# Block products in the first feed-forward layer as well, modulation rows moved, border squares summed by products, two output tiles together in the recurrent output: a float32 decoder trunk on one core

## Chip, cores, metric

One core of one Trainium2 chip. The metric is the time of one launch on the device in microseconds; the median of several runs counts. All inputs lie in device memory, the output is written there.

## What is computed

Two layers over a sequence of 512 tokens, model width 1024. Layer 0 mixes by sparse attention, layer 1 by a gated recurrent unit; each is followed by a feed-forward block of 22 x 128 = 2816 hidden units. Everything is float32.

```python
def swiglu(h, w_in, w_out):
    g, u = jnp.split(h @ w_in, 2, axis=-1)
    return (jax.nn.silu(g) * u) @ w_out

def reference(x, c, ada_w, ada_b, ...):
    cond = jax.nn.silu(c)
    for layer in range(DEPTH):
        mod = (cond @ ada_w[layer] + ada_b[layer])[:, None, :]
        sh1, sc1, g1, sh2, sc2, g2 = jnp.split(mod, 6, axis=-1)
        hh = rms_norm(x, norm1_g[layer]) * (1.0 + sc1) + sh1
        ...
        x = x + g1 * mix        # mix: nsa_mixer in layer 0, rglru_mixer in layer 1
        hh = rms_norm(x, norm2_g[layer]) * (1.0 + sc2) + sh2
        x = x + g2 * swiglu(hh, ffn_w_in[layer], ffn_w_out[layer])
    return x
```

## The kernel before

Activations lie transposed: `x` is eight tiles of 128 features x 512 tokens. Every float32 factor is split into a high part and a low rest of a reduced type (`split`, L244), and a product is three matmuls, high x high, high x low, low x high (`mm3`, L256 to L261). A weight tile of 128 x 1024 is loaded raw into one of four buffers `wraw` (`raw`, L216), ScalarE makes the high halves (L248), DVE or POOL the low ones (L254), into six buffers each. `chunk` (L230) does both halves and then `behind` (L223), which issues up to `per_chunk` modulation rows of a list `todo`.

A **modulation row** (`ada`, L264) is one of 96 tiles of 512 KB of `ada_w`: its load goes through `raw`, DVE multiplies it by the broadcast condition and sums (L271), and adds a bias of 128 x 1 (L272).

The program in order: `setup` (condition, masks); `nsa`, which starts with the squares of `x`, the normalising scale (`norm_scale`, L298: sums of squares by small products L309, a power on POOL L278, a diagonal L318, its broadcast by PE L320) and a loop over the eight input tiles (L601) with 24 products of 512 columns for each; then the selection and compression branches and attention, with the last output projection in token halves (`w_out_last`, L1080) as the border to the next block; `ffn(0)`; `rg`; `ffn_blocks(1)`.

The plain `ffn` (L520) takes hidden tiles in pairs (gate and value), 24 products of 512 columns each, Silu at L540. `ffn_blocks` (L377) computes a pair by a two-by-two block scheme with seven products in place of eight: 7 x 4 x 3 = 84 matmuls of 256 columns. `load(j)` (L398) brings the pair's two raw tiles `v` and `g` and makes sums and differences on DVE (L404 to L407); `run(i, j)` (L418) does one of the seven products, with its weight split just before, and the outputs are put together on DVE (L430, L444 to L450). Silu of the first half stands at L431. The right operands are made once per layer by `right_operands` (L354, differences L360). Two pairs at the head are done whole, since the blocks need all of the operands.

`project_out` (L547) multiplies the hidden tiles by the output weights; with `ahead` = 2 the first two output tiles are done together, hidden tile by hidden tile. `sq_add` (L281) squares a finished tile on ScalarE and adds it to the running sum on POOL, except those in `apart`, which stay for a product of their own.

A scheduler sets the order on each engine from the order of the program and the numbers in `PRIORITY` (L122); an engine works its list in order, and loads are issued by SP in the order of its own list.

Of the kernel before, what the change touches and what calls it, by code (L numbers as in the profile page):

```python
# [105 lines left out]
class Build:  # L106
    def __init__(self, ctx, tc, ins, out):
# [15 lines left out]
        "ada1": -140, "ada2": -20, "ck": -60, "cmp": -60, "comb": 90, "exp": -170, "fill": -6, "first2": -40,  # L123
        "first4": -20, "gates": -60, "gproj": -25, "krms": -20, "kt": 60, "late": 30, "lo": -300, "max": 20,
        "mod1": -100, "mod2": 40, "mod3": -66, "nsc1": -41, "nsc2": -40, "pres3": -20, "psplit": 10, "pv": 15,
# [36 lines left out]
    def setup(self):  # L162
        nc, c = self.nc, self.const
        row = self.raw(self.ins["c"], D)[:1]
        self.load_x()
        self.vec = c.tile([128, NVEC], F32, name="vec")
        nc.sync.dma_start(self.vec, self.ins["vec"])
        self.ones = c.tile([128, 128], F32, name="ones")
        nc.vector.memset(self.ones, 1.0)
        nc.scalar.activation(row, row, AF.Silu)  # L170
        self.cond = c.tile([128, D], F32, name="cond")
        for h in range(2):
            b = self.bank()
            nc.tensor.matmul(b, self.ones[:1], row[:, 512 * h:512 * h + 512], start=True, stop=True)
            nc.scalar.activation(self.cond[:, 512 * h:512 * h + 512], b, AF.Copy)
        self.mhalf = c.tile([128, 16], F32, name="mhalf")
# [26 lines left out]

    def load_x(self, behind=None):
        self.x = []
        for n in range(KT):
            self.x.append(self.slot("A", name="x"))
            d = self.nc.sync.dma_start(self.x[n], self.ins["x"][:, n])
            if behind is not None:
                self.after(d.ins, behind.ins.name)  # L210

# [51 lines left out]

    def ada(self, l, m, n, engine):  # L264
# [5 lines left out]
        w = self.raw(self.ins["ada_w"][l, KT * m + n], D)  # L270
# [26 lines left out]
    @step("nsc")  # L297
    def norm_scale(self, cs=ALL, behind=None):  # L298

# [18 lines left out]
        nc.vector.tensor_tensor(dg, self.ident[:, None, :].to_broadcast([128, nt, 128]),  # L318
                                r[:, :, None].to_broadcast([128, nt, 128]), op=OP.mult)
        nc.tensor.matmul(R[:, :w], self.ones, dg.rearrange("p a b -> p (a b)"), start=True, stop=True)  # L320
        return R[:, :w]

    def hh_tile(self, n, R, A, B, cs=ALL, to=None, t=None):
        nc = self.nc
        if t is None:
            t = self.slot("T")[:, cs]
        nc.vector.tensor_tensor(t, self.x[n][:, cs], R, op=OP.mult)
# [21 lines left out]

    BLOCKWISE = ((1, 2),)  # L350
    kept = {}
# [25 lines left out]
    def ffn_blocks(self, l, last):  # L377
# [20 lines left out]
        def load(j):  # L398
# [4 lines left out]
            with self.pri("wsum"):  # L403
# [48 lines left out]


        plain = dict(zip((0, HT, 1), self.first(src, (0, HT, 1))))
        if l == 0:
            self.rg_prepare()
        w = self.chunk(src[HT + 1], 1024)
        self.right_operands()
        plain[HT + 1] = self.bank()
        for k in range(KT):  # L460
            self.mm3(plain[HT + 1], w[128 * k:128 * k + 128], self.hh[k], k == 0, k == KT - 1)
        for j in (0, 1):
# [12 lines left out]
        run(4, HT - 1)  # L475
        self.flush((l, 5))
        for j in range(HT):
# [69 lines left out]
    def project_out(self, src, h, gate, then, ahead=1):  # L547
# [34 lines left out]
    def nsa(self):  # L582
        nc, tc = self.nc, self.tc
        for n in range(KT):
            self.sq_add(n, nc.vector, apart=(6,))
        for m in (0, 1):
            last = self.ada(0, m, 0, nc.vector)
        R = self.norm_scale(behind=last)
        with tc.tile_pool(name="nsa", bufs=1) as np_:
            self.np_ = np_  # L590

            self.K = {g: [self.slot("K", F32R, f"K{g}", self.KW) for _ in range(2)] for g in range(GROUPS)}
            self.V, self.qs, self.oT, self.cells, self.ends = {}, {}, {}, [], []
# [7 lines left out]
            for k in range(KT):  # L601
                for m in (0, 1) if k else ():
                    self.ada(0, m, k, nc.vector)
                A = self.make_A(0, 1, slice(k, k + 1))
                hh.append(self.hh_tile(k, R, A, self.mod[0, 0]))
                w = self.chunk(self.ins["nsa_w1"][k], 1024, "ag")
                for t in range(4):
                    s = slice(128 * t, 128 * t + 128)
                    self.mm3(cb[t], w[s], hh[k], k == 0, k == KT - 1)
                for i in range(NT):  # L610
                    s = slice(128 * i, 128 * i + 128)
                    self.mm3(wb[i], (hh[k][0][:, s], hh[k][1][:, s]),
                             w[512:1024], k == 0, k == KT - 1)
            self.todo += [(0, m, n) for m in (2, 4, 3) for n in range(KT)]
            self.behind_on = nc.vector
# [464 lines left out]
    def w_out_last(self, cs):  # L1080
# [3 lines left out]
        for n in range(KT):  # L1084
# [37 lines left out]
    def rg(self):  # L1122
        nc, tc = self.nc, self.tc
        src = self.ins["rg_in"]
        early = dict(zip((RT, RT + 1, RT + 2), self.first(src, (RT, RT + 1, RT + 2))))

# [204 lines left out]
```

## Time and profile before

| | |
|---|---|
| median of 3 runs | 1368.15 us (1366.61 to 1369.36) |
| profiled execution | 1366.38 us, its span 1364.5 us |
| PE busy | 1306.9 us, 96%, 7423 instructions |
| PE weight loads | 1113.4 us, 82% |
| DVE busy | 931.2 us, 68% |
| ScalarE busy | 702.6 us, 51% |
| POOL busy | 239.8 us, 18% |
| mean granted TensorE clock | 0.991 |

The span runs from the first to the last instruction of the profiled execution; 1.9 us of its time lie around it. By the trace the loop over the input tiles of attention runs from 23 to 72 us, the border from 384 to 411, `ffn(0)` from 407 to 766, the recurrent block to 1011 and `ffn_blocks(1)` to the end. A matmul's printed time overlaps the next one's, so the distance of starts is what a stream of them costs. A clock of 1.00 stands for 2.4 GHz, 0.5 for 1.2 GHz.

### The profile page before, as it was taken

How to read it: one execution, taken by the hardware profiler on the slowest of the kernel's cores; microseconds unless marked ns; L12 is line 12 of the kernel's file. 1: busy time of each engine (PE TensorE's matmuls, PEld its weight loads, DVE VectorE, ACT ScalarE, POOL GpSimd, SP SyncE). 2: the span in 40 equal slices, each digit the busy share in tenths (PEclk: the TensorE clock that was granted, in tenths of full speed). 3: DMA queues.
4: the chain of work that ended last, by engine and by line, in shares of the span. 5: the costliest groups of instructions: out<-in, count | busy, mean ns of one | idle time of the engine just before them, and what ended most of it. 6: DMA issues, size and time to landing. Idle time of an engine off the chain costs nothing.

```text
span 1364.5 us, 20521 instructions
## 1 busy us (share of the span) xinstructions
PE 1306.9 (96%) x7423; PEld 1113.4 (82%) x7423; DVE 931.2 (68%) x1883; ACT 702.6 (51%) x1605; POOL 239.8 (18%) x334
## 2 busy tenths in 40 slices
PE   5989988899989999999999999999999999999998
PEld 4789866667769888888888987787898999998887
DVE  7885987888877566566533577478369888887331
ACT  4473588888665333333222555595366555556221
POOL 3540334586341000000000013300110000000000
PEclk9999999999999999999999999999999999999999
DMA  7667600210214666666643123222322333334430
GB/s 261 227 189 241 218 21 1 92 64 17 84 56 140 215 201 203 194 191 191 196 131 101 63 85 93 93 93 85 101 78 89 98 97 118 96 96 126 123 112 24
DMA packets 50071, 167.20 MB, mean 123 GB/s; under 512 B 5553, under 2 KB 6833, under 8 KB 49970
## 3 DMA queue, kind: packets, MB, share of 16 engines
q1 hardware_dynamic: 49970, 165.90, 39.3%
q8 instruction: 58, 0.95, 0.3%
q14 instruction: 43, 0.35, 0.1%
HBM read 163.78 MB, written 2.10 MB: 122 GB/s over the span
## 4 chain that ended last, share of the span: by engine, by line
PE 77%; DVE 11%; issue 4%; ACT 4%; DMA 2%; POOL 2%; POOLq 0%; SPq 0%; ACTq 0%; DVEq 0%
PE bank_tr L259 9%; PE bank_tr L260 9%; PE bank_tr L261 9%; PE bank_sc L259 7%; PE bank_sc L260 7%; PE bank_sc L261 7%; PE bank_mm L259 4%; PE bank_mm L260 4%; PE bank_mm L261 4%; PE bank_pv L261 3%; PE bank_pv L259 2%; PE bank_pv L260 2%; PE bank_tr L1046 2%; PE bank_pv L1059 2%; DVE wraw L271 2%
## 5 line engine op out<-in xcount | busy, mean ns | idle before, releaser
L248 ACT ACTIVATE whi<-wraw 128x512 fp32r<-128x512 f32 (+4 forms) x422 | 245.4, 594 | 424.0 <-PE bank_tr L260 152.4
L254 DVE TENSOR_TENSOR wlo<-wraw,whi 128x512 fp32r<-128x512 f32 (+3 forms) x390 | 254.3, 658 | 183.4 <-ACT whi L248 174.2
L271 DVE SCALAR_TENSOR_TENSOR wraw<-wraw,cond 128x1024 f32<-128x1024 f32 x96 | 119.1, 1241 | 73.9 <-DMA wraw<-in_ada_w 73.5
L259 PE MATMUL bank_tr<-hh,whi 128*128 128x512 f32 (+1 forms) x400 | 137.3, 344 | 5.3 <-ACT hh L248 3.0
L261 PE MATMUL bank_tr<-hh,wlo 128*128 128x512 f32 (+1 forms) x400 | 135.5, 339 | 1.8 <-DVE wlo L254 1.8
L260 PE MATMUL bank_tr<-hh,whi 128*128 128x512 f32 (+1 forms) x400 | 136.3, 341 | 0.1
L295 POOL TENSOR_TENSOR sq<-sq 128x256 f32<-128x256 f32 (+1 forms) x25 | 25.9, 1034 | 432.2 <-ACT sq L286 431.8
L261 PE MATMUL bank_sc<-hh,wlo 128*128 128x512 f32 (+1 forms) x284 | 101.1, 356 | 0.0
L259 PE MATMUL bank_sc<-hh,whi 128*128 128x512 f32 (+1 forms) x284 | 101.1, 356 | 0.0
L260 PE MATMUL bank_sc<-hh,whi 128*128 128x512 f32 (+1 forms) x284 | 101.1, 356 | 0.0
L259 PEld LDWEIGHTS bank_tr<-hh,whi 128*128 128x128 f32 x400 | 76.5, 191 | 17.8 <-ACT hh L248 4.7
L261 PEld LDWEIGHTS bank_tr<-hh,wlo 128*128 128x128 f32 x400 | 76.6, 192 | 10.0 <-DVE wlo L254 2.0
L260 PEld LDWEIGHTS bank_tr<-hh,whi 128*128 128x128 f32 x400 | 76.7, 192 | 8.8 <-DVE hh L254 0.6
L1011 DVE TENSOR_REDUCE nm<-bank_sc 128x1 f32<-128x32 f32 (+4 forms) x192 | 69.5, 383 | 14.1 <-PE bank_sc L970 8.3
L995 POOL TENSOR_SCALAR p<-p,rr 128x128 f32<-128x128 f32 (+3 forms) x128 | 66.4, 539 | 45.5 <-DVE rr L986 36.6
L1014 ACT ACTIVATE p<-bank_sc,nm 128x384 f32<-128x384 f32 (+3 forms) x128 | 67.2, 531 | 11.6 <-DVE nm L1011 10.9
L248 ACT ACTIVATE ph<-bank_tr 128x512 fp32r<-128x512 f32 (+1 forms) x96 | 56.0, 595 | 14.6 <-PE bank_tr L1046 13.4
L1046 PE MATMUL bank_tr<-ident,p 128*128 128x128 f32 x320 | 55.1, 276 | 5.9 <-DVE ph L254 4.9
L261 PEld LDWEIGHTS bank_sc<-hh,wlo 128*128 128x128 f32 x284 | 53.9, 190 | 8.0 <-DVE wlo L254 0.4
L259 PEld LDWEIGHTS bank_sc<-hh,whi 128*128 128x128 f32 x284 | 53.9, 190 | 7.6 <-ACT whi L248 0.2
L260 PEld LDWEIGHTS bank_sc<-hh,whi 128*128 128x128 f32 x284 | 53.8, 189 | 7.5
L254 POOL TENSOR_TENSOR wlo<-wraw,whi 128x512 fp32r<-128x512 f32 (+1 forms) x44 | 53.4, 1227 | 32.9 <-ACT whi L248 32.5
(429 smaller groups left out, 3712.2 us busy)
## 6 DMA issues: line engine op xcount, KB each, us to landing
wraw<-in_ada_w SPq DMA_DIRECT2D x96, 512.0 KB, 4.2
wraw<-in_ffn_in SPq DMA_DIRECT2D x88, 512.0 KB, 3.7
wraw<-in_ffn_out SPq DMA_DIRECT2D x32, 512.0 KB, 3.6
wraw<-in_rg_in SPq DMA_DIRECT2D x22, 512.0 KB, 3.3
wraw<-in_ffn_out SPq DMA_DIRECT2D x16, 384.0 KB, 3.1
x<-in_x SPq DMA_DIRECT2D x16, 256.0 KB, 3.9
wraw<-in_nsa_w SPq DMA_DIRECT2D x8, 512.0 KB, 4.5
wraw<-in_cmp_w SPq DMA_DIRECT2D x8, 512.0 KB, 5.1
```

The costliest lines, as they stand in the source:

```text
L248: nc.scalar.activation(hi, full, AF.Copy)
L254: e.tensor_tensor(lo, full, hi.bitcast(F32), op=OP.subtract)
L259: a = mm(out, w[0], x[0], start=first, stop=False)
L260: mm(out, w[0], x[1], start=False, stop=False)
L261: return a, mm(out, w[1], x[0], start=False, stop=last)
L271: done = engine.scalar_tensor_tensor(w, w, 1.0, self.cond, op0=OP.mult, op1=OP.mult, accum_out=mod)
L295: engine.tensor_tensor(s, s, t, op=OP.add)
L995: nc.gpsimd.tensor_scalar(P[br, h], P[br, h], r[:, h, x:x + 1], 1.0, op0=OP.mult, op1=OP.mult)
L1011: nc.vector.tensor_reduce(nm[:, h, x:x + 1], b[:, cols[br]] if len(brs) > 1 else b, axis=AX, op=OP.max, negate=True)
L1014: nc.scalar.activation(dst, b[:, cols[br]] if len(brs) > 1 else b, AF.Exp, bias=nm[:, h, x:x + 1], accum_out=sm[:, h, x:x + 1])
L1046: nc.tensor.transpose(t[:n, 128 * h:128 * h + 128], srcs[h], self.ident)
L1059: mm(o, V[:, g], ph, start=first and u == 0, stop=False)
```

## The change

- `ffn_blocks(0)` takes the place of `ffn(0)`. Both layers now do three pairs whole (`PLAIN`), and the first two block pairs are interleaved. Layer 0 issues a modulation row with every odd pair; in layer 1 none are left.
- The start: two modulation rows load among the tiles of `x`, into the eight `K` buffers; the squares are summed by PE alone; products of no use (`warm`) run on PE ahead of the first ones needed; the low halves of the loop over input tiles move from POOL to DVE.
- The border: `w_out_last` keeps squares 2 to 7 apart, so PE sums them by products.
- `per_chunk` is 0 in most of `rg`, and 1 in the gate projection and from the third output tile on; the recurrent output is called with `ahead` = 2.

```diff
 def setup(self):
-        self.load_x()
+        self.x, self.early = [], []
+        for n in range(KT):
+            self.x.append(self.slot("A", name="x"))
+            nc.sync.dma_start(self.x[n], self.ins["x"][:, n])
+            if n >= KT - 2:
+                self.early.append(self.raw(self.ins["ada_w"][0, KT * (n - KT + 2)], D, True))
...
+        nc.scalar.activation(self.cond[:, 0:1], self.ones[:, 0:1], AF.Silu)
+        self.warm(8, self.ones)
...
+    def warm(self, n, src):
+        for _ in range(n):
+            self.nc.tensor.matmul(self.idle_bank[:, :128], self.ones, src[:, :128], start=True, stop=True)
...
-    def raw(self, src, w):
-        t = self.wp.tile([128, 1024], F32, name="wraw", bufs=4)
+    def raw(self, src, w, wide=False):
+        t = self.slot("K", name="adaw", w=1024) if wide else self.wp.tile([128, 1024], F32, name="wraw", bufs=4)
...
 def norm_scale(self, cs=ALL, behind=None, warm=None):
...
+        if warm:
+            self.after(d.ins, warm[0].ins.name)
+            self.warm(warm[1], parts[-1])
+        m = nc.tensor.matmul(R[:, :w], self.ones, dg.rearrange("p a b -> p (a b)"), start=True, stop=True)
...
-    BLOCKWISE = ((1, 2),)
+    BLOCKWISE = ((0, 2), (1, 2))
+    PLAIN = (3, 3)
...
-            if j % 2:
+            if j % 2 and l == 0:
                 self.behind()
...
+        n = self.PLAIN[l]
...
-        for j in range(2, HT):
+        load(n)
+        run(1, n)
+        run(2, n)
+        load(n + 1)
+        for i, j in ((1, n + 1), (2, n + 1), (5, n), (6, n), (3, n), (7, n), (5, n + 1), (4, n), (6, n + 1), (3, n + 1),
+                     (7, n + 1)):
+            run(i, j)
+        for j in range(n + 2, HT):
             load(j)
             for i in (1, 2, 5):
                 run(i, j)
-            if j > 2:
-                run(4, j - 1)
+            run(4, j - 1)
             for i in (6, 3, 7):
                 run(i, j)
         run(4, HT - 1)
-        self.flush((l, 5))
...
 def project_out(...):
+            self.per_chunk = 1 if n0 > 1 or K > 16 else 0
...
 def nsa(self):
-            self.sq_add(n, nc.vector, apart=(6,))
-        for m in (0, 1):
-            last = self.ada(0, m, 0, nc.vector)
-        R = self.norm_scale(behind=last)
+            self.sq_add(n, nc.vector, apart=range(1, KT))
+        first, last = [self.ada(0, m, 0, nc.vector, self.early[m]) for m in (0, 1)]
+        R = self.norm_scale(behind=first, warm=(last, 6, 0))
...
-                    self.ada(0, m, k, nc.vector)
+                    d = self.ada(0, m, k, nc.vector, self.raw(self.ins["ada_w"][0, KT * m + k], D, True))
...
-                w = self.chunk(self.ins["nsa_w1"][k], 1024, "ag")
+                w = self.chunk(self.ins["nsa_w1"][k], 1024)
...
 def w_out_last(self, cs):
-            self.sq_add(n, self.nc.gpsimd, cs)
+            self.sq_add(n, self.nc.gpsimd, cs, range(2, KT))
...
 def rg(self):
+        self.per_chunk = 0
...
+        self.per_chunk = 1
         with self.pri("gproj"):
             gb = [project(j) for j in range(8)]
+        self.per_chunk = 0
...
-        self.project_out(self.ins["rg_out"][0], y, self.mod[1, 2], (1, 2))
+        self.project_out(self.ins["rg_out"][0], y, self.mod[1, 2], (1, 2), 2)
...
-        self.ffn(0, False)
+        self.ffn_blocks(0, False)
```

How it moves instructions, at three places. First DVE at the start, from the last sum of squares to the first scaled tile; L271, L287 multiply a modulation row, `nv` is the mean square, L318, L334 the diagonal. Before:

```order
L295 TENSOR_TENSOR sq<-sq 128x512 [waits DVE_49,Activation_49] x4
L295 TENSOR_TENSOR sq<-sq 128x512 [waits Activation_49]
...
L271 SCALAR_TENSOR_TENSOR wraw,mod_154<-wraw,cond 128x1024 [waits DMAHW2_49,Activation_49]
L272 TENSOR_TENSOR mod_154<-mod_154,vec 128x1 [waits DVE_49]
L271 SCALAR_TENSOR_TENSOR wraw,mod_159<-wraw,cond 128x1024 [waits DMAHW3_49]
L313 TENSOR_SCALAR nv<-bank_sc 128x4 [waits PE_49]
L272 TENSOR_TENSOR mod_159<-mod_159,vec 128x1 [waits DVE_49]
L511 SCALAR_TENSOR_TENSOR A_203<-mod_159,vec 128x1 [waits DVE_49]
L318 TENSOR_TENSOR slotT<-ident,rs_r 128x512 [waits Pool_49]
```

And now:

```order
L287 SCALAR_TENSOR_TENSOR adaw,mod_161<-adaw,cond 128x1024 [waits DMAHW0_49,Activation_49]
L329 TENSOR_SCALAR nv<-bank_sc 128x4 [waits PE_49]
L287 SCALAR_TENSOR_TENSOR adaw,mod_164<-adaw,cond 128x1024 [waits DMAHW2_49]
L288 TENSOR_TENSOR mod_161<-mod_161,vec 128x1 [waits DMAHW3_49,DVE_49]
L334 TENSOR_TENSOR slotT<-ident,rs_r 128x512 [waits Pool_49]
L288 TENSOR_TENSOR mod_164<-mod_164,vec 128x1 [waits DVE_49]
```

No sums of squares are left on DVE, and the mean square stands ahead of the second modulation row.

Second DVE in the first feed-forward block, a stretch with one modulation row. Before, in plain pairs:

```order
L254 TENSOR_TENSOR wlo<-wraw,whi 128x512 [waits DMAHW3_49,PE_49,Activation_49]
L541 TENSOR_TENSOR slotT<-slotT,bank_pv 128x512 [waits PE_49]
L254 TENSOR_TENSOR wlo<-wraw,whi 128x512 [waits Activation_49]
L271 SCALAR_TENSOR_TENSOR wraw,mod_5873<-wraw,cond 128x1024 [waits DMAHW0_49]
L254 TENSOR_TENSOR h<-slotT,h 128x512 [waits Activation_49]
```

And now, around the second product of an odd pair (L455 and L475 end two products, L429 to L432 are the pair's sums and differences):

```order
L472 TENSOR_TENSOR f<-f,s 128x256 [waits DVE_49]
L269 TENSOR_TENSOR wlo<-wraw,whi 128x512 [waits PE_49,Activation_49]
L287 SCALAR_TENSOR_TENSOR wraw,mod_6058<-wraw,cond 128x1024 [waits DMAHW0_49]
L455 TENSOR_TENSOR f<-bank_tr,st 128x256 [waits PE_49,Activation_49]
L429 TENSOR_TENSOR ws<-wraw 128x512 [waits DMAHW7_49]
L288 TENSOR_TENSOR mod_6058<-mod_6058,vec 128x1 [waits DVE_49]
L269 TENSOR_TENSOR wlo<-wraw,whi 128x512 [waits DMAHW6_49,Activation_49]
L475 TENSOR_TENSOR f<-f,bank_tr 128x256 [waits PE_49]
L430 TENSOR_TENSOR ws<-ws,wraw 128x512 [waits DVE_49]
```

The row's multiplication, which waits for its load, stands ahead of the pair's sums and of its further low halves.

Third POOL at the border, from the first token half's last sums to the second's power operation. Before:

```order
L254 TENSOR_TENSOR oT<-slotT,oT 128x128 [waits Activation_49] x2
L295 TENSOR_TENSOR sq<-sq 128x256 [waits Activation_49,Pool_49] x3
L278 TENSOR_TENSOR rs_r<-nv,mhalf 128x2 [waits DVE_49]
L295 TENSOR_TENSOR sq<-sq 128x256 [waits PE_49,Activation_49]
L295 TENSOR_TENSOR sq<-sq 128x256 [waits Activation_49,Pool_49] x5
```

And now:

```order
L311 TENSOR_TENSOR sq<-sq 128x256 [waits Activation_49,Pool_49]
L269 TENSOR_TENSOR oT<-slotT,oT 128x128 [waits Activation_49] x2
L294 TENSOR_TENSOR rs_r<-nv,mhalf 128x2 [waits DVE_49]
L311 TENSOR_TENSOR sq<-sq 128x256 [waits PE_49,Activation_49]
L294 TENSOR_TENSOR rs_r<-nv,mhalf 128x2 [waits DVE_49]
```

One sum of two squares a half is left on POOL; the other six go to PE, where each pair of small products waits for ScalarE's square alone.

## Rows read from the trace of the kernel before

**Rows 1.** Page, the chain that ended last, by engine.
```profile
PE 77%; DVE 11%; issue 4%; ACT 4%; DMA 2%; POOL 2%; POOLq 0%; SPq 0%; ACTq 0%; DVEq 0%
```
**Rows 2.** Windows, core 0: us, then busy us (instructions) of each engine; clock, DMA share, GB/s.
```profile
core 0: us, PE busy (x) PEld busy (x) DVE busy (x) ACT busy (x) POOL busy (x), PEclk, DMA share, GB/s
550.00:600.00 50.00, 50.00 (x223) 41.40 (x222) 30.53 (x59) 16.49 (x27) 0.00 (x0) 1.00 0.66 194
1100.00:1150.00 50.00, 50.00 (x412) 49.15 (x411) 41.48 (x79) 28.32 (x59) 0.00 (x0) 1.00 0.36 106
1012.00:1036.00 24.00, 21.50 (x149) 20.08 (x150) 23.72 (x55) 18.84 (x37) 0.00 (x0) 0.99 0.14 44
...
404.00:411.00 7.00, 5.06 (x24) 5.06 (x25) 6.13 (x17) 5.70 (x15) 3.35 (x4) 0.52 0.30 87
```
**Rows 3.** Timeline of ScalarE in the plain block (start us, us, instruction).
```profile
514.43 0.58 ACT L540 ACTIVATE slotT<-bank_mm 128x512 f32<-128x512 f32 x1
...
644.99 0.58 ACT L540 ACTIVATE slotT<-bank_mm 128x512 f32<-128x512 f32 x1
```
**Rows 4.** All of line 431: ns min/median/max, first and last start.
```profile
L431 ACT ACTIVATE f<-f x20: 401/402/417, 1038.3 to 1233.4; 128x256 f32<-128x256 f32 x20
```
**Rows 5.** Timeline of PE, start to key scale; in brackets the idle time before.
```profile
18.55 2.08 PE L320 MATMUL bank_tr<-slotT,ones 128*128 128x512 f32 x2 [3.52 <-DVE slotT L318]
23.13 1.22 PE L259 MATMUL bank_tr<-hh,whi 128*128 128x512 f32 x2 [2.50 <-ACT hh L248]
...
27.56 0.63 PE L261 MATMUL bank_pv<-hh,wlo 128*128 128x512 f32 x1
27.99 0.60 PE L261 MATMUL bank_mm<-whi,hh 128*128 128x512 f32 x1
...
39.24 0.50 PE L259 MATMUL bank_tr<-hh,whi 128*128 128x512 f32 x1 [2.01 <-DVE slotT L327]
...
86.59 0.60 PE L260 MATMUL bank_tr<-wlo,hh 128*128 128x280 f32 x1 [4.01 <-POOL wlo L254]
```
**Rows 6.** Timeline of DVE at the start.
```profile
14.31 1.22 DVE L271 SCALAR_TENSOR_TENSOR wraw<-wraw,cond 128x1024 f32<-128x1024 f32 x1
...
16.75 1.75 DVE L318 TENSOR_TENSOR slotT<-ident,rs_r 128x512 f32<-128x512 f32 x1 [0.82 <-POOL rs_r L278]
...
20.82 0.68 DVE L327 TENSOR_TENSOR slotT<-x,bank_tr 128x512 f32<-128x512 f32 x1
...
40.85 0.15 DVE L272 TENSOR_TENSOR mod<-mod,vec 128x1 f32<-128x1 f32 x1
...
42.07 0.08 DVE L271 DVE_READ_ACCUMULATOR wraw<-wraw,cond 128x1 f32 x1
42.18 1.12 DVE L272 TENSOR_TENSOR mod<-mod,vec 128x1 f32<-128x1 f32 x1
```
**Rows 7.** Page, costliest groups: POOL's low halves (busy us, mean ns).
```profile
L254 POOL TENSOR_TENSOR wlo<-wraw,whi 128x512 fp32r<-128x512 f32 (+1 forms) x44 | 53.4, 1227 | 32.9 <-ACT whi L248 32.5
```
**Rows 8.** Timeline of PE, head of the second feed-forward block.
```profile
1035.30 0.55 PE L261 MATMUL bank_tr<-hh,wlo 128*128 128x256 f32 x1 [1.82 <-DVE wlo L254]
```
**Rows 9.** Two lines on DVE: ns min/median/max, first and last start.
```profile
L360 DVE TENSOR_TENSOR xt<-xb x4: 416/416/417, 1018.4 to 1027.8; 128x256 f32<-128x256 f32 x4
...
L1113 DVE TENSOR_SCALAR rgp<-rgp x8: 168/172/173, 427.2 to 432.1; 128x11 f32<-128x11 f32 x8
```
**Rows 10.** Page, loads: KB each, median us from issue to landing.
```profile
wraw<-in_ada_w SPq DMA_DIRECT2D x96, 512.0 KB, 4.2
```
**Rows 11.** Timelines of POOL, ScalarE, DVE and PE at the border.
```profile
400.42 5.47 POOL L295 TENSOR_TENSOR sq<-sq 128x256 f32<-128x256 f32 x6 [0.69 <-ACT sq L286]
...
402.30 0.40 ACT L286 ACTIVATE sq<-x 128x256 f32<-128x256 f32 x1
...
404.63 0.67 DVE L254 TENSOR_TENSOR hh<-slotT,hh 128x256 fp32r<-128x256 f32 x1
...
405.94 1.87 PE L309 MATMUL bank_sc<-ones,sq 128*128 128x1 f32 x8 [4.52 <-POOL sq L295]
```
**Rows 12.** Waits of PE in the recurrent output: us in total, times, longest.
```profile
PE bank_mm L259 <- ACT yh L248: 0.7, 2, 0.5
```

More of the change, by code (lines that the diff above doesn't have):

```diff
@@ L123 @@
         "ada1": -140, "ada2": -20, "ck": -60, "cmp": -60, "comb": 90, "exp": -170, "fill": -6, "first2": -40,
-        "first4": -20, "gates": -60, "gproj": -25, "krms": -20, "kt": 60, "late": 30, "lo": -300, "max": 20,
+        "first4": -20, "gates": -60, "gproj": -25, "idle": -40, "krms": -20, "kt": 60, "late": 30, "lo": -300, "max": 20,
         "mod1": -100, "mod2": 40, "mod3": -66, "nsc1": -41, "nsc2": -40, "pres3": -20, "psplit": 10, "pv": 15,
@@ L169, in setup @@
         nc.vector.memset(self.ones, 1.0)
-        nc.scalar.activation(row, row, AF.Silu)
         self.cond = c.tile([128, D], F32, name="cond")
+        b = [self.bank("sc") for _ in range(2)]
+        self.idle_bank = self.bank("mm")
+        nc.scalar.activation(self.cond[:, 0:1], self.ones[:, 0:1], AF.Silu)
+        self.warm(8, self.ones)
         for h in range(2):
-            b = self.bank()
-            nc.tensor.matmul(b, self.ones[:1], row[:, 512 * h:512 * h + 512], start=True, stop=True)
-            nc.scalar.activation(self.cond[:, 512 * h:512 * h + 512], b, AF.Copy)
+            nc.tensor.matmul(b[h], self.ones[:1], row[:, 512 * h:512 * h + 512], start=True, stop=True)
+        for h in range(2):
+            nc.scalar.activation(self.cond[:, 512 * h:512 * h + 512], b[h], AF.Silu)
         self.mhalf = c.tile([128, 16], F32, name="mhalf")
@@ L202, in setup, with load_x @@
         self.mod = {}
-    def load_x(self, behind=None):
+    def warm(self, n, src):
+        for _ in range(n):
+            self.nc.tensor.matmul(self.idle_bank[:, :128], self.ones, src[:, :128], start=True, stop=True)
+    def load_x(self, behind):
         self.x = []
@@ L208, in load_x @@
             d = self.nc.sync.dma_start(self.x[n], self.ins["x"][:, n])
-            if behind is not None:
-                self.after(d.ins, behind.ins.name)
+            self.after(d.ins, behind.ins.name)
     def v(self, name, i, n=1):
         return self.vec[:, VEC[name] + i:VEC[name] + i + n]
-    def raw(self, src, w):
-        t = self.wp.tile([128, 1024], F32, name="wraw", bufs=4)
+    def raw(self, src, w, wide=False):
+        t = self.slot("K", name="adaw", w=1024) if wide else self.wp.tile([128, 1024], F32, name="wraw", bufs=4)
         d = self.nc.sync.dma_start(t[:src.shape[0], :w], src)
@@ L261, in mm3, with ada @@
         return a, mm(out, w[1], x[0], start=False, stop=last)
-    def ada(self, l, m, n, engine):
+    def ada(self, l, m, n, engine, w=None):
         nc = self.nc
@@ L269, in ada @@
         mod = self.mod[l, m][:, n:n + 1]
-        w = self.raw(self.ins["ada_w"][l, KT * m + n], D)
+        if w is None:
+            w = self.raw(self.ins["ada_w"][l, KT * m + n], D)
         done = engine.scalar_tensor_tensor(w, w, 1.0, self.cond, op0=OP.mult, op1=OP.mult, accum_out=mod)
@@ L297, in norm_scale @@
     @step("nsc")
-    def norm_scale(self, cs=ALL, behind=None):
+    def norm_scale(self, cs=ALL, behind=None, warm=None):
         nc = self.nc
@@ L317, in norm_scale @@
         dg = self.slot("T")[:, :w].rearrange("p (a b) -> p a b", a=nt)
-        nc.vector.tensor_tensor(dg, self.ident[:, None, :].to_broadcast([128, nt, 128]),
-                                r[:, :, None].to_broadcast([128, nt, 128]), op=OP.mult)
-        nc.tensor.matmul(R[:, :w], self.ones, dg.rearrange("p a b -> p (a b)"), start=True, stop=True)
+        d = nc.vector.tensor_tensor(dg, self.ident[:, None, :].to_broadcast([128, nt, 128]),
+                                    r[:, :, None].to_broadcast([128, nt, 128]), op=OP.mult)
+        if warm:
+            self.after(d.ins, warm[0].ins.name)
+            self.warm(warm[1], parts[-1])
+        m = nc.tensor.matmul(R[:, :w], self.ones, dg.rearrange("p a b -> p (a b)"), start=True, stop=True)
+        if warm:
+            with self.pri("idle"):
+                self.warm(warm[2], dg.rearrange("p a b -> p (a b)"))
         return R[:, :w]
@@ L326, in hh_tile @@
             t = self.slot("T")[:, cs]
-        nc.vector.tensor_tensor(t, self.x[n][:, cs], R, op=OP.mult)
+        d = nc.vector.tensor_tensor(t, self.x[n][:, cs], R, op=OP.mult)
+        if n == 0:
+            self.first_hh = d
         nc.scalar.activation(t, t, AF.Identity, bias=B[:, n:n + 1], scale=A[:, n:n + 1])
@@ L456, in ffn_blocks @@
             self.rg_prepare()
-        w = self.chunk(src[HT + 1], 1024)
+        more = [(t, self.chunk(src[t], 1024)) for t in (HT + 1,)]
         self.right_operands()
[L459 to L462, printed above, removed]
+        for t in [t for j in range(2, n) for t in (j, HT + j)]:
+            more.append((t, None))
+        for t, w in more:
+            plain[t] = self.bank()
+            w = w or self.chunk(src[t], 1024)
+            for k in range(KT):
+                self.mm3(plain[t], w[128 * k:128 * k + 128], self.hh[k], k == 0, k == KT - 1)
+        for j in range(n):
             f = self.slot("B", name="f")
@@ L602, in nsa @@
                 for m in (0, 1) if k else ():
-                    self.ada(0, m, k, nc.vector)
+                    d = self.ada(0, m, k, nc.vector, self.raw(self.ins["ada_w"][0, KT * m + k], D, True))
+                    if k == 1:
+                        self.after(d.ins, self.first_hh.ins.name)
                 A = self.make_A(0, 1, slice(k, k + 1))
                 hh.append(self.hh_tile(k, R, A, self.mod[0, 0]))
-                w = self.chunk(self.ins["nsa_w1"][k], 1024, "ag")
+                w = self.chunk(self.ins["nsa_w1"][k], 1024)
                 for t in range(4):
@@ L613, in nsa @@
                              w[512:1024], k == 0, k == KT - 1)
+            self.K = {g: [self.slot("K", F32R, f"K{g}", self.KW) for _ in range(2)] for g in range(GROUPS)}
             self.todo += [(0, m, n) for m in (2, 4, 3) for n in range(KT)]
```

1 line of the change is left out of this document (removed).

## Prediction

> **What bounds the kernel now.** I read the chain of waits first: PE carries 77% of it and DVE 11% [rows 1], so time goes when PE has less to stream or stands idle less. Then the busy time by stretch [rows 2]: in both feed-forward stretches PE is busy all 50 us of 50, so there only the number and length of matmuls counts. But DVE, at 30.53 of 50 us under whole tiles, is at 41.48 under block products, and PE's weight loads go from 41.40 to 49.15: the block form buys PE time with DVE time. Third come the rows of the places where PE stands idle: the start, the border after attention, the head of the second feed-forward block. DVE there is busy 23.72 us of 24 [rows 2]; that stall is DVE's making. The sum is made against the profiled execution, 1366.4 us (1.8 under the median of the runs). A run of this kernel can be told from no change from about 0.2%, 2.7 us.
>
> **Feed-forward pairs.** A pair is two hidden tiles of 128. Whole, it is 48 matmuls of 512 columns; the period is (644.99 - 514.43) / 12 = 10.88 us [rows 3], 227 ns a matmul. By blocks it is 84 of 256 columns: 20 Silus from 1038.3 to 1233.4, 19 periods of 10.27 us [rows 4], 122 ns each. So 0.61 us a pair. FFN0 turns 19 of its 22 pairs: -11.6. FFN1 makes one pair more whole: +0.6. **-11.0.**
>
> That counts DVE and the loads at nothing. What hides them: by blocks DVE is busy 41.48 us of 50 [rows 2], 8.50 a pair, 17.0 in two pairs of 20.5. FFN0 adds one modulation row on every odd pair: 1.22 + 0.08 + 0.15 = 1.45 [rows 6], so 18.45 of 20.5; 2.05 are left. The row's 512 KB also take one of the four raw buffers, so its load can only be issued once an earlier pair's second tile has been split, takes 4.2 us [rows 10], and everything behind it in DVE's queue (second order listing: the block's sums, the low halves) waits. By the chain split (4, j-2), row landed, row multiplied, next first tile landed and split, that is 4.2 + 1.2 + 4.2 + 1.3 = 10.9 us from about the middle of pair j-1 to the start of pair j+1, 16 us: it fits with some 5 to spare. I take no loss; the rivals have the other end.
>
> **Heads of both blocks.** FFN1's head loses 1.82 us to a low half on DVE [rows 8] and about as much to the half clock behind it. It gets two more whole tiles, 2 x 24 x 0.227 = 10.9 us of PE work, for some 4 us of DVE work: the stall should go, **-3.5** (bounds -4 and 0). In FFN0 the same head stands with the recurrent block's small operations (17 of 0.17 us [rows 9] or a little less, interleaved) and the differences of the block operands: between the low half of the fourth tile and that of the fifth DVE has 12 differences of 0.42 [rows 9], about 0.34 apart, 6 splits of 0.6 and those 17, some 9.5 to 10, and PE has one tile, 5.4, and what it lags. By that PE would wait some 1.5 us: **+1.5** (0 to +5).
>
> **Start.** Before, the scale waits for both first modulation rows; now for one (first order listing): the second one's 1.22 and its 0.08 [rows 6] leave the path. The diagonal took 1.75 us [rows 6] with POOL's low halves running; with POOL idle I take 0.6, near the 0.68 of a 512-column product [rows 6]. The broadcast took 2.08 us at half clock [rows 5], half of it if the warm-up products do what they are for. That is -3.5 for the first product, now at 23.13 [rows 5]. From there 12 matmuls stood 0.43 us apart [rows 5] instead of 0.227: -2.4. The wait of 2.01 us at 39.24 [rows 5] came from a DVE that small operations slowed (the same 128x1 addition 0.15 and 1.12 [rows 6]) while POOL made low halves of 1.23 us mean [rows 7]. These 16 go to DVE at 0.6 each; per input tile DVE then has 2 x 1.45 + 0.15 + 0.6 + 3 x 0.6 = 5.45 us against PE's 24 x 0.227 = 5.44. So the wait may go (-2.0), but nothing is left over. Against it: the key scale's power operation now stands ahead of a further pair of POOL's low halves, the wait of 4.01 us at 86.59 [rows 5] may grow by about 1.4. **-6.5**, bounds -9 and -1 (no warm clock, DVE late).
>
> **Border.** POOL adds seven squares one after another, six in 5.47 us from 400.42 [rows 11], and PE stands 4.52 us before 405.94 [rows 11]; ScalarE had the last square at 402.30 + 0.40 [rows 11]. Now PE sums them by 14 small products as they come. PE's next bound is the first block input, whose low half DVE begins at 404.63 [rows 11]. The first block product came 1.87 us after the wait's end, 407.8 [rows 11], now about 405, and half of the slow stretch behind it (clock 0.52 from 404 to 411 [rows 2]) goes: **-3.5** (-5.5 to -1.5; its T buffers hold seven squares now, which could delay one).
>
> **Recurrent output.** Two output tiles together take each gated tile every 1.36 us instead of 0.68; waits on its halves are 0.7 us [rows 12] and the restarts behind them as much. Eight modulation rows move into the gate projection, 8 x 1.45 = 11.6 us on DVE, beside PE. **-1** (-2 to +1).
>
> Sum: -11.0 - 3.5 + 1.5 - 6.5 - 3.5 - 1 = -24.0: profile 1342.4, median 1344. Attention, which neither gains nor loses an instruction, is counted at nothing.
>
> **A rule against it.** The trace has 227 ns for 512 columns and 122 for 256 in this very program [rows 3, 4]: nearly half. The Trainium skill, "TensorE: Matmul & The Clock Gate", section "Back-to-back issue gap", puts a sustained stream of weight load and matmul at about 131 ns for 512 columns and 81 for 128, so that narrow ones are dear; a line between gives an estimate of 98 ns at 256, a pair of 8.2 us by blocks against 6.3 whole, and the 19 pairs would cost 37 us instead of saving. The trace does not agree with either number, and the measurement decides.
>
> **Rivals.**
> A. The start does not pay: PE's clock is still half at the first product, or DVE's 5.45 us an input tile are late from the first. For: nothing is left over. Then -1 instead of -6.5: 1349.5. Chance 0.17.
> B. A modulation row's landing stands in DVE's queue for up to one load time in two pairs. For: a load takes 4.2 us [rows 10] and nothing behind the row on DVE can pass it; against: the chain above has 5 us to spare. One whole landing: 18.45 + 4.2 = 22.65 against 20.5, +2.15 in each of 9.5 double pairs, +20: 1364. A part of it lies between. Chance 0.10, of that 0.04 within 0.2%.
> C. **Slower:** two landings, the modulation row's and that of the next pair's first tile, which waits for its buffer, stand there one after the other: 18.45 + 8.4 = 26.85, +6.35 in each of 9.5, +60: 1404. It decides against the change from (24 / 9.5) + 2.05 = 4.6 us of waiting in two pairs. Place: the row's multiplication ahead of the block's sums. For: four buffers, and 4.2 us a load [rows 10]; against: FFN1 runs the same loop with 1.8 us of DVE idle a pair. Chance 0.07.
> D. The spacing of 256 columns carries a larger fixed part in FFN0. Weight loads are at 49.15 of 50 us in the block stretch [rows 2]. If a third of the 227 ns were fixed, 256 columns would take 151 ns, a pair 12.7 us, 19 pairs +35: 1390; the point is 10.88 / 84 = 130 ns. This is the rule above; the rows with 122 speak against it. Chance 0.01.
> E. The blocks in FFN0 bring nothing, since a pair settles at 10.88: 1356. Chance 0.02.
>
> **The numbers.** 0.63 stays for the forecast, 1344. The range goes down to the good ends of start, border and output (-4.5 for the first two, -1 for the last, -5.5 together, and -4 of both heads: 1333) and up to B short of its end, 1362. Faster by over 0.2%: 0.63 + 0.17 + 0.06 + 0.02 = 0.88; within: 0.04; slower: 0.07 + 0.01 = 0.08.
>
> **What would show it.** Silu rows of FFN0 10.3 us apart, with PE busy in the whole stretch and DVE near 45 of 50. The first product near 19.5 us with 0.23 between matmuls; no wait at 39; the input tiles done some 8 us earlier than before. PE idle under 3 us at the border and the recorded clock up again within a few products; no wait of DVE's making at FFN1's first blocks. The prediction is wrong if FFN0's pairs take 10.9 or more, with DVE rows that wait for a load of modulation rows or of weights, or if the start's gain is back by the key scale.

## The result and the profile after

The changed kernel takes 1357.24 us (median of 5 runs, 1354.63 to 1360.85), the kernel before 1369.36 in the same comparison: a ratio of 0.9915, 95% interval 0.9891 to 0.9939. It is 12 us faster; 24 were forecast. The profiled execution took 1354.63 us, its span is 1352.9.

Page of the changed kernel, busy time and chain (before: [rows 1]):

```profile
PE 1314.0 (97%) x8187; PEld 1151.1 (85%) x8187; DVE 1024.5 (76%) x2115; ACT 754.0 (56%) x1739; POOL 212.3 (16%) x308
...
PE 75%; DVE 10%; DMA 5%; issue 4%; ACT 4%; POOL 2%; POOLq 0%; SPq 0%; DVEq 0%; ACTq 0%
```

DVE has 93 us more work, PE 7 more (the small and the idle products are counted), and loads are on the chain with 5%. Where the time went is read from the starts, on PE, of the first product of each stage in both traces:

| stage, on PE | before, us | after, us | difference | forecast |
|---|---|---|---|---|
| start to first transpose of keys | 96.52 | 95.13 | -1.4 | -6.5, with the next |
| from there to the first scores | 63.03 | 65.05 | +2.0 | |
| attention, scores to last transpose | 225.69 | 227.13 | +1.4 | 0 |
| border, to the first product of FFN0 | 22.43 | 19.67 | -2.8 | -3.5 |
| FFN0 with its output, to the recurrent block | 366.16 | 359.18 | -7.0 | -10.1 |
| recurrent block to its output | 165.35 | 165.74 | +0.4 | 0 |
| recurrent output to FFN1 | 66.13 | 65.07 | -1.1 | -1 |
| FFN1 | 354.84 | 351.63 | -3.2 | -2.9 |

FFN0 and FFN1 are the two feed-forward layers; the forecast of FFN0 is its 19 pairs and its head, -11.6 + 1.5. Four lines are near the forecast. The start gave nothing, FFN0 less, and attention, whose instructions and order did not change, took 1.4 more. Each column is one profile. Among this profile and those of the experiments, the ones with the same instructions in a stage spread there by 2.0 us in FFN0 (358.6 to 360.6; three with another order on PE reach 363.3), 1.2 in the border (19.7 to 20.9) and 0.5 in FFN1 (351.5 to 352.1): the gain in FFN1 is firm, those in FFN0 and the border are known to that much.

**The start.** Timeline of PE after (before: [rows 5]):

```profile
6.53 12.71 PE L325 MATMUL bank_sc<-ones,sq 128*128 128x1 f32 x64
19.10 2.91 PE L217 MATMUL bank_mm<-sq,ones 128*128 128x128 f32 x12
22.31 2.04 PE L339 MATMUL bank_mm<-slotT,ones 128*128 128x512 f32 x2 [0.31 <-DVE qg L630]
26.71 1.65 PE L274 MATMUL bank_tr<-hh,whi 128*128 128x512 f32 x3 [2.35 <-ACT hh L263]
...
30.29 0.63 PE L275 MATMUL bank_tr<-hh,whi 128*128 128x512 f32 x1
30.71 0.63 PE L276 MATMUL bank_tr<-hh,wlo 128*128 128x512 f32 x1
...
32.77 0.39 PE L275 MATMUL bank_sc<-wlo,hh 128*128 128x512 f32 x1
33.01 0.40 PE L276 MATMUL bank_sc<-whi,hh 128*128 128x512 f32 x1
```

The 32 products that sum the squares (64 records, two for each) take 12.71 us, 0.40 each, and the last square was done at 13.1. The first useful product stands at 26.71, 3.6 us later than before, and its followers are still 0.42 apart. The way to it goes over the mean square `nv` on DVE, POOL's power operation, the diagonal on DVE and the broadcast on PE. Before:

```profile
15.46 0.15 DVE L313 TENSOR_SCALAR nv<-bank_sc 128x4 f32<-128x4 f32 x1
15.70 1.02 POOL L278 TENSOR_TENSOR rs_r<-nv,mhalf 128x4 f32<-128x4 f32 x1 [12.94 <-DVE nv L313]
```

After, with ScalarE's last square on top:

```profile
12.49 0.63 ACT L302 ACTIVATE sq<-x 128x512 f32<-128x512 f32 x1 [1.32 <-DMA x<-in_x]
19.27 0.16 DVE L329 TENSOR_SCALAR nv<-bank_sc 128x4 f32<-128x4 f32 x1 [6.12 <-PE bank_sc L325]
19.52 1.93 POOL L294 TENSOR_TENSOR rs_r<-nv,mhalf 128x4 f32<-128x4 f32 x1 [16.73 <-DVE nv L329]
21.48 0.69 DVE L334 TENSOR_TENSOR slotT<-ident,rs_r 128x512 f32<-128x512 f32 x1 [0.83 <-POOL rs_r L294]
```

The mean square comes 3.8 us later. The power operation takes 0.9 more, with DVE's multiplication of the second row beside it (19.35 to 20.57), the diagonal 1.1 less, and the broadcast is as long as before, 2.04 against 2.08: together 3.6. The last square is done 1.1 us later than before, too: it waits for the last tile of `x`, in front of whose load a modulation row was put. The clock (windows with the columns of [rows 2]):

```profile
10.00:15.00 5.00, 5.00 (x25) 5.00 (x25) 1.24 (x2) 1.75 (x3) 0.00 (x0) 0.50 1.04 411
```

PE is busy all the time there, with products of one column, and its clock is granted at 0.50, 1.2 GHz.

What came after was better than before: no wait at 39, and only 0.67 us on POOL's low half in place of 4.01. So the first transpose of keys comes 1.4 us earlier, but after a new wait on DVE's values, and with a stretch at half clock behind it (PE's timeline; the window from 95 to 100 us):

```profile
83.94 0.40 PE L275 MATMUL bank_tr<-wlo,hh 128*128 128x280 f32 x1 [0.67 <-POOL wlo L269]
95.13 0.33 PE L733 MATMUL bank_tr<-ident,kn 128*128 128x128 f32 x1 [1.85 <-DVE V L725]
```
```profile
95.00:100.00 5.00, 4.87 (x27) 4.86 (x28) 3.87 (x9) 1.38 (x2) 1.21 (x2) 0.66 0.89 304
```

That took the 1.4 back before the first scores. In the profiles of e6, e8, e9, e10 and e11 (below) the clock stayed up there, and the stretch from the keys to the scores took 62.8 to 63.5 us; in this one, e1, e5 and e7 it fell and the stretch took 64.7 to 66.0, and in e2, e3 and e12 it fell again between 112 and 160 us (0.93 to 0.96) and the stretch took 66.9 to 69.8. The change in the kernel does not decide it: e8 and e12 have the same start.

**FFN0.** Timelines of ScalarE and DVE, and DVE's waits from 460 to 620 us (us in total, times, longest):

```profile
467.76 0.40 ACT L456 ACTIVATE f<-f 128x256 f32<-128x256 f32 x1
478.93 0.42 ACT L456 ACTIVATE f<-f 128x256 f32<-128x256 f32 x1 [0.55 <-DVE f L455]
488.58 0.40 ACT L456 ACTIVATE f<-f 128x256 f32<-128x256 f32 x1
...
634.83 0.40 ACT L456 ACTIVATE f<-f 128x256 f32<-128x256 f32 x1
```
```profile
498.27 1.22 DVE L287 SCALAR_TENSOR_TENSOR wraw<-wraw,cond 128x1024 f32<-128x1024 f32 x1 [1.75 <-DMA wraw<-in_ada_w]
```
```profile
DVE wraw L287 <- DMA wraw<-in_ada_w: 11.7, 7, 1.8
```

Sixteen pairs take (634.83 - 467.76) / 16 = 10.44 us each, in turn about 11.2 and 9.65, where FFN1's take 10.24. In the odd pairs DVE waits up to 1.8 us for the modulation row, then multiplies it, with the block's sums behind.

**The border.** PE no longer waits for POOL [rows 11], but sums for 3.29 us, at full clock 0.235 a product:

```profile
403.83 3.29 PE L325 MATMUL bank_sc<-ones,sq 128*128 128x1 f32 x28
```

### The profile page after: what moved, and what is told of

Its sections match the earlier page's. It is cut to its first block, busy times and chain, and to the rows that moved or that the text cites. A ratio compares the mean times of both kernels' runs of the same rounds, so it can differ in the third digit from the quotient of the medians.

```text
span 1352.9 us, 22420 instructions
## 1 busy us (share of the span) xinstructions
PE 1314.0 (97%) x8187; PEld 1151.1 (85%) x8187; DVE 1024.5 (76%) x2115; ACT 754.0 (56%) x1739; POOL 212.3 (16%) x308
## 4 chain that ended last, share of the span: by engine, by line
PE 75%; DVE 10%; DMA 5%; issue 4%; ACT 4%; POOL 2%; POOLq 0%; SPq 0%; DVEq 0%; ACTq 0%
PE bank_tr L274 9%; PE bank_tr L275 8%; PE bank_tr L276 8%; PE bank_sc L274 7%; PE bank_sc L276 7%; PE bank_sc L275 7%; PE bank_mm L274 4%; PE bank_mm L276 4%; PE bank_mm L275 4%; DMA wraw<-in_ada_w 3%; PE bank_tr L1084 2%; DVE wlo L269 2%; PE bank_pv L274 2%; PE bank_pv L275 2%; PE bank_pv L276 2%
## 5 line engine op out<-in xcount | busy, mean ns | idle before, releaser
L287 DVE SCALAR_TENSOR_TENSOR wraw<-wraw,cond 128x1024 f32<-128x1024 f32 x80 | 99.0, 1238 | 54.2 <-DMA wraw<-in_ada_w 54.0
L274 PE MATMUL bank_tr<-hh,whi 128*128 128x256 f32 (+1 forms) x396 | 123.6, 317 | 2.8 <-ACT hh L263 2.8
L275 PE MATMUL bank_tr<-hh,whi 128*128 128x256 f32 (+1 forms) x396 | 122.7, 310 | 0.0
L276 PE MATMUL bank_tr<-hh,wlo 128*128 128x256 f32 (+1 forms) x396 | 122.2, 309 | 0.0
L274 PE MATMUL bank_tr<-xs,whi 128*128 128x256 f32 x340 | 96.6, 284 | 0.7 <-DVE f L455 0.6
L276 PE MATMUL bank_tr<-xs,wlo 128*128 128x256 f32 x340 | 95.8, 282 | 0.0
L275 PE MATMUL bank_tr<-xs,whi 128*128 128x256 f32 x340 | 95.8, 282 | 0.0
L263 ACT ACTIVATE whi<-ws 128x512 fp32r<-128x512 f32 x114 | 71.7, 631 | 37.6 <-ACT st L464 17.5
L276 PE MATMUL bank_sc<-hh,wlo 128*128 128x256 f32 (+1 forms) x252 | 81.8, 324 | 0.6 <-DVE wlo L269 0.6
L274 PE MATMUL bank_sc<-hh,whi 128*128 128x256 f32 (+1 forms) x252 | 81.7, 324 | 0.0
L275 PE MATMUL bank_sc<-hh,whi 128*128 128x256 f32 (+1 forms) x252 | 81.1, 322 | 0.0
L269 DVE TENSOR_TENSOR wlo<-ws,whi 128x512 fp32r<-128x512 f32 x114 | 77.9, 685 | 1.1 <-ACT whi L263 0.9
L1052 ACT ACTIVATE p<-bank_sc,nm 128x384 f32<-128x384 f32 (+3 forms) x128 | 67.2, 531 | 11.6 <-DVE nm L1049 10.9
L274 PEld LDWEIGHTS bank_tr<-xs,whi 128*128 128x128 f32 x340 | 64.5, 190 | 2.2 <-DVE f L455 1.5
```

What stands on the lines that cost most here:

```text
L263: nc.scalar.activation(hi, full, AF.Copy)
L269: e.tensor_tensor(lo, full, hi.bitcast(F32), op=OP.subtract)
L274: a = mm(out, w[0], x[0], start=first, stop=False)
L275: mm(out, w[0], x[1], start=False, stop=False)
L276: return a, mm(out, w[1], x[0], start=False, stop=last)
L1052: nc.scalar.activation(dst, b[:, cols[br]] if len(brs) > 1 else b, AF.Exp, bias=nm[:, h, x:x + 1], accum_out=sm[:, h, x:x + 1])
```

## The experiments

Each median is that of its runs; ratios are to the kernel before in the same comparison. In single profiles attention differs by several us (last section), so parts are judged by their own stages.

**e1, squares of x on DVE.** In `nsa`:
```diff
-            self.sq_add(n, nc.vector, apart=range(1, KT))
+            self.sq_add(n, nc.vector, apart=(6,))
```


> Undoes one part of the start alone: the eight squares of x are added on DVE again (two small products groups on PE instead of eight), all else as in the change. Theory S (the 32 small products with one column, 12.7 us on PE in the changed kernel's trace, hold the mean square until 19.27): the mean square comes at about 15.6 us, the first product at 22.8 instead of 26.7, the time is 3 to 4 us under the change, some 1353 to 1354. Rival L (the loads: a modulation row of 512 KB went in front of the last tile of x): the first product stays within 1 us of 26.7 and the time does not move.

1352.22 us, 0.9882 (0.9861 to 0.9903).

```profile
16.11 0.16 DVE L329 TENSOR_SCALAR nv<-bank_sc 128x4 f32<-128x4 f32 x1 [1.96 <-PE bank_sc L325]
```
```profile
23.55 0.80 PE L274 MATMUL bank_tr<-hh,whi 128*128 128x512 f32 x1 [2.35 <-ACT hh L263]
```

The mean square comes 3.2 us earlier, the first product too. S holds; L falls as the cause of these 3.2 us. But a part of it is there: in e1 the last square is done at 13.4 us, before at 12.1, and the first product still comes 0.4 us later than before (23.13), with the squares on DVE in both.

**e4, the whole start as before** (`setup` and `nsa` of the kernel before).


> The whole start, up to the loop over input tiles with its low halves on POOL, as in the kernel before; all the rest as in the change. Theory S says that the start as changed gained nothing: the first score products of attention come within 0.5 us of 161, time within 1 us of the change (1356 to 1358). If the start did gain (or lose) something that the profile hides, such as the clock later in attention, the time moves by over 2 us.

1359.01, 0.9921 (0.9897 to 0.9946); the first scores at 159.97, against 160.18 with the change. The start as changed was worth nothing, by the stage and by the time.

**e8 and e5, products of no use: none, or wide.** e8 takes them away from e1; e5 puts these in their place, six behind the last square product and five behind the broadcast:
```diff
+            d = self.nc.tensor.matmul(to, self.identb, self.mask[:, :512], start=True, stop=True)
+            self.after(d.ins, behind.ins.name)
```


> As e1_squares_dve, without any products of no use. If they do nothing, the first product stays at 23.5 us, the half clock lasts as long (until about 28.8 us) and the time stays within 1 us; if they help at all, the half clock lasts longer or the first product comes later.

> As e1_squares_dve, with the products of no use made wide: six of 512 columns (16-bit) between the last square product and the broadcast and five behind it, in place of the six of 128 columns. [...] Rival (the clock cannot be brought up so early by anything on PE): 12 to 13 first products at 0.43 us as before, same time as e1_squares_dve.

e8: 1350.96, 0.9881 (0.9858 to 0.9905), first product at 23.77, in e1 23.55: without the 128-column products nothing is lost that the time can tell. e5 was to have the first useful products 0.23 us apart and the end of the loop 2 to 3 us earlier than e1. 1351.86, 0.9872 (0.9848 to 0.9895). Its PE timeline:

```profile
20.09 2.05 PE L345 MATMUL bank_mm<-slotT,ones 128*128 128x512 f32 x2 [0.50 <-DVE qg L636]
...
24.48 0.96 PE L279 MATMUL bank_tr<-hh,whi 128*128 128x512 f32 x3 [0.87 <-ACT hh L268]
...
25.52 0.39 PE L280 MATMUL bank_tr<-hh,whi 128*128 128x512 f32 x1
25.75 0.39 PE L281 MATMUL bank_tr<-hh,wlo 128*128 128x512 f32 x1
```

The useful products are 0.23 apart from the first, as expected. That came with the five behind the broadcast: behind the first six the broadcast took 2.05 us, as long as in e1, and the wait ahead of the first useful product is 0.87 us here, 2.35 in e1 and e8. Whether the width, the 16-bit type or the filling of that wait kept the clock up, no run takes apart; a full clock came behind 128-column products too (last section). From the first product to the keys it is 66.55 us, in e8 68.13. But the first came 0.7 later here, the keys 1.4 earlier than in e1, and of the rest nothing can be told in the time.

**e2 and e6, fewer modulation rows among FFN0's blocks.** e2 takes `self.behind()` out of `load` and flushes layer 0's rows ahead of the output projection. e6 is e1 with
```diff
-            if j % 2 and l == 0:
+            if j in (5, 13) and l == 0:
...
         for j in range(RT):
+            self.per_chunk = 1 if 2 <= j < 10 else 0
             conv(j)
```


> No modulation row is issued among the block pairs of the first feed-forward layer; the ten rows come later, two before the output projection, the others behind it. Theory M (the row on DVE delays every odd pair): all pairs take 10.25 us, as in layer 1, instead of 10.44 on average, so 16 to 19 times 0.19 = 3 to 3.5 us less in that stretch, time 1354 to 1355 if the moved rows cost nothing elsewhere. Rival (the first layer's pairs are long for another reason, such as its loads or operands): pairs stay at 9.65 and 11.3 in turn and the time stays.

> As e1_squares_dve, but only two modulation rows stand among the block pairs (pairs 5 and 13); the eight others go with the convolution tiles of the recurrent block. Theory M (each row delays its pair by DVE, 0.3 to 0.35 us for each of the pairs): pairs without a row take 10.25 us, the block stretch is 3 to 4.5 us shorter than in e1_squares_dve, the output projection's head stays as it is, the recurrent stretch grows by under 0.5 us: time 1348 to 1349.5. Rival (what the blocks save comes back in the recurrent block or the output projection, as in e2_no_rows_in_blocks): time within 1 us of e1_squares_dve.

e2: 1367.78, 0.9991 (0.9974 to 1.0008): the whole gain is gone. Yet FFN0 from its first product to the first of its output went from 232.85 to 230.16 us, 2.7 for the ten rows; M holds, a little under the 3 to 3.5 expected. It came back twice: two rows ahead of the output's hidden halves let PE wait, with a stretch at half clock behind,

```profile
642.98 0.59 PE L276 MATMUL bank_mm<-h,wlo 128*128 128x512 f32 x1 [3.72 <-DVE wlo L269]
```

and rows left over to the recurrent output, 14 in place of 8, made that stage 72.24 us, not 65.07. e6: 1359.86, 0.9935 (0.9917 to 0.9953); pairs 10.25, the odd one with a row 11.3, and 230.79 us up to the output in place of e1's 233.67; but the recurrent block, from its first product with the tiles `us`, took 149.9 us instead of 141.5, about 1 us a row. Neither the theory nor the rival had the time: both kernels are slower, by the medians e2 10.5 us than the change and e6 7.6 than e1.

**e9, e10, the eight rows in FFN0's output.** e9 is e1 with rows in pairs 5 and 13 and
```diff
-            self.per_chunk = 1 if n0 > 1 or K > 16 else 0
+            self.per_chunk = (2 if n0 > 4 else 1) if K > 16 else int(n0 > 1)
```
e10 has e5's wide products as well.


> As e1_squares_dve, with two modulation rows among the block pairs (5 and 13) and the eight others in the output projection of the first feed-forward block, two with each weight tile of its last three output tiles. Theory M with room (DVE is busy 18 of 40 us from 720 to 760 in the changed kernel, so rows cost nothing there): the stretch from the first block product to the recurrent block is 3 us shorter than in e1_squares_dve, the recurrent stretch stays at 141.5 us (it was 149.9 with the rows in it): time 1348 to 1350. Rival (a row costs about 1 us wherever it goes): the output projection grows by 3 us or more, same time as e1_squares_dve.

> As e9_rows_in_output, with the wide products of no use of e5_wide_warm. If both act in their own stretches, the end of the first loop comes 1.5 to 2.5 us earlier than in e9_rows_in_output, all later stretches as there: time 1346 to 1349, the best of these kernels. If attention takes the start's gain back, within 1 us of e9_rows_in_output.

e9: 1351.01, 0.9877 (0.9855 to 0.99). FFN0 with its output took 358.33 us, in e1 360.17: 1.8 gained of 3, which is within the spread of that stage; the recurrent block stayed at 140.6. e10: 1353.06, 0.9876 (0.9861 to 0.989): the keys come 0.6 us earlier than in e9, but the same rows made a wait at the very end of the output, with a stretch at half clock behind, 4.5 us together:

```profile
750.39 0.39 PE L281 MATMUL bank_pv<-h,wlo 128*128 128x256 f32 x1 [2.20 <-DVE wlo L274]
```

In e9's profile, with the same instructions there, PE does not wait for a low half: two rows a weight tile are near the bound.

**e3, e7, the border.** e3 drops `range(2, KT)`; e7 has `range(4, KT)`. The text on record calls e7 "the change"; its kernel has e1's squares as well, so e1 is its comparison.


> The border's squares are added on POOL again, all else as in the change. Theory B (the small products saved 2.6 us of span between the last attention transposes and the first block product): the border gets 2 to 3 us longer, PE waits 4.5 us for POOL again, time 1359 to 1360. Rival (the border's gain in the profile is chance of the clock): the time stays within 1 us.

> As the change, but squares 1 to 3 of each border half are added on POOL and 4 to 7 by products, half of the added products. Theory B (28 records at 0.117 us, 3.3 us, stand on PE ahead of the first block product): the border is 1 to 1.5 us shorter than the change, if POOL's three sums (0.9 us each) are done when PE comes to them. Rival (POOL's chain again holds PE): the border is as long or longer.

e3: 1361.11, 0.9939 (0.9919 to 0.9958), border 21.98 against 19.67 us, outside the 19.7 to 20.9 of the ten profiles with the change's border: B holds, 2.3 us in these two. Its PE waits again:

```profile
411.36 1.87 PE L325 MATMUL bank_sc<-ones,sq 128*128 128x1 f32 x8 [4.07 <-POOL sq L311]
```

e7: 1351.01, 0.9869 (0.9844 to 0.9893), border 19.43 against e1's 20.05: 0.6, less than the 1 expected and less than the spread. A gain is not shown.

**e11, recurrent output singly** (the last argument of `project_out` left out).


> As the change, with the recurrent output's first two tiles one after the other, as before. Theory: two together save about 1 us between the first product of that output and the second feed-forward block (65.07 against 66.13 us), so that stretch goes back to 66 and the time rises by 1 us at most, which the runs can hardly tell. Rival (that difference comes from the modulation rows moved away): the stretch stays at 65.

1361.42, 0.9939 (0.9916 to 0.9963); the stage took 70.44 us, 5.4 more than with the change. PE waits for DVE and ScalarE, and its clock falls to 0.66 from 940 to 950:

```profile
938.39 0.50 PE L275 MATMUL bank_tr<-yl,whi 128*128 128x512 f32 x1 [0.58 <-DVE yl L269]
941.65 0.80 PE L274 MATMUL bank_tr<-yh,whi 128*128 128x512 f32 x1 [2.53 <-ACT yh L263]
```

Before, the same order took 66.13, and the last modulation row was multiplied at 690 us; now eight are in the recurrent block and eight in its output, here one of them just ahead of the low half that PE waits for at 938:

```profile
936.50 1.22 DVE L287 SCALAR_TENSOR_TENSOR wraw<-wraw,cond 128x1024 f32<-128x1024 f32 x1
```

So moving rows about cost some 4.3 us here, which two tiles together covered; the net of -1.1 hid both. That the moved rows are what cost it is inferred, no run has tiles singly with rows as before.

**e12, parts together:** e1, e8, e7's border, two rows among the blocks, eight in the third to fifth output tile.


> The parts that looked best, put together: squares of x on DVE, no products of no use, squares 1 to 3 of each border half on POOL, two modulation rows among the block pairs and the eight others in the third to fifth output tile of the first feed-forward block (away from its end, where e10_rows_and_wide had a wait of 2.4 us). If the stretches add up: first product 23.6, block stretch 190.4, output projection 126 to 126.5, border 19.5: time 1347 to 1350. If rows in the output projection cost even there: output projection 128 or more and time as e1_squares_dve, 1352.

1349.43, 0.9848 (0.9824 to 0.9872): the lowest median, though its interval overlaps those of e1, e5, e7, e8, e9 and e10. Output 126.3 and border 19.4 as expected, and from the first product of the block scheme to the output 189.40, where 190.4 was expected. (That product stands 22 places later in PE's order than in the change, whose 194.77 is therefore no measure for it.) FFN0 with its output takes 355.74 us, 3.4 less than in the change. By the medians it is 8 us under the change; its profile lost 4.8 us between the keys and the scores (69.82).

## Why the prediction was wrong

The sign and the range held; the size did not, 12 us against 24.

- **Start: wrong.** The step that failed is "-3.5 for the first product": it took away the second modulation row, the slow diagonal and half of the broadcast, but gave the squares by PE alone no price at all. The trace of before had it:

```profile
11.46 3.57 PE L309 MATMUL bank_sc<-ones,sq 128*128 128x1 f32 x16 [4.18 <-DVE sq L295]
```

Eight products in 3.57 us, wait for the last square included, 0.45 each. Thirty-two of them at that price are 14 us; they took 12.71, and e1 shows that 3.2 us of the mean square's delay are theirs. Of its three terms the diagonal held (-1.1). The second row could not give its 1.3: it ran beside these products, which end at 15.03 by the same line, 0.4 us ahead of the mean square at 15.46. The broadcast gave nothing. Two more terms were left out, the later last square (1.1) and the power operation, 0.9 longer with the changed start in every run and 1.02 us again with the old one (e4); that the row beside it is the reason no run shows alone. "-2.4" for the clock failed too: with the change's products of no use or without them (e8) the first useful ones were 0.42 apart, behind e5's wide ones 0.23. "-2.0" for the wait at 39 held, and POOL's low half, priced as +1.4, fell to 0.67 us instead. What was won to the keys was given back by the half clock behind the wait on DVE's values. Rival A named the right end, no gain from the start, and only half the cause.
- **FFN0's pairs:** 0.44 a pair instead of 0.61. "I take no loss" was wrong: rival B came in part, 1.8 us of landing in each odd pair where 4.2 was its end. By its own account 18.45 + 1.75 is still under 20.5; that fits an overrun not of DVE's total but of what stands behind the row, the sums for the fifth product; no run took them apart. The head cost 0.67 of 1.5, but the output's start lost 0.95 to DVE, which was not counted.
- **FFN1's head, border, recurrent output:** -3.2, -2.8, -1.1 for -2.9, -3.5, -1. In the border the term left out was the same as at the start, small products on PE, 3.3 us there. The output's net was right by chance (e11): the working counted the eight rows beside the gate projection, not the eight in the output itself.
- **Rival D**, wide and narrow products: 10.25 us a pair in FFN0 without rows (e6) and 10.24 in FFN1 leave it no place.
- **The range:** its low end counts both heads at -4, where their bounds leave -2, and starts from the profile; by its own bounds it is 1336.5, not 1333. At 1357 it made no difference.

## What to carry over

A float32 matmul of one column is not free, 0.24 us at full clock and 0.40 to 0.45 at half here; an operation that is moved to another engine is to be priced by that engine's own row, also where the engine looks idle. Work that waits for a load does not belong ahead of the bound engine's supplies on an in-order queue; where it costs nothing has to be found stage by stage, since the same rows cost nothing that shows in the first layer's output (e12), about 0.3 us each among the blocks (e2, e6) and 1 in the recurrent block (e6). And a step taken off a chain gives back only the time up to the next thing that the chain waited for, as the second row did.

## What was not expected

PE was busy without a break from 6.5 to 22 us, with one-column and 128-column products, and its clock was granted at half, up to 31.7 us. In e2 and e11, with the same products in the same order, it was granted at 1.00 from 22 to 25 us; the broadcast took 1.10 us, and behind the wait of 2.35 us the clock was at half again (e11, timeline and windows):

```profile
22.25 1.10 PE L339 MATMUL bank_mm<-slotT,ones 128*128 128x512 f32 x2 [0.31 <-DVE qg L630]
```
```profile
22.00:25.00 3.00, 1.10 (x2) 0.30 (x2) 2.60 (x8) 0.81 (x1) 0.00 (x0) 1.00 1.03 412
25.50:28.50 3.00, 2.81 (x7) 2.23 (x8) 3.00 (x9) 1.18 (x3) 0.00 (x0) 0.50 1.03 410
```

So it was in four of the eight profiles with the 128-column products (e7 and e9 are the others); without them (before, e4, e8, e12) the broadcast took 2.07 or 2.08 us. What decides it is not shown. A wait on PE could cost as much again: behind those at 95 us here (1.85), 643 in e2 (3.72), 750 in e10 (2.20) and 941 in e11 (2.53) a stretch at half clock followed, the first worth about 2 us by the profiles without it. Attention, with the same instructions in the same order on PE, took from 223.7 to 230.1 us in these profiles, with the clock from 155 to 240 us between 0.90 and 0.98, and no edit touched it: so the totals of two single profiles tell nothing under 6 us, and the runs of one kernel (e11) spread over 16.
